# Two SwiGLU stages of a decoder layer: gate and up columns by seven block products over all of K, with one pool of raw weight buffers per stage

## The chip, the core and the metric

The kernel runs on one core of a Trainium2 chip. The core has five engines with instruction streams of their own: TensorE (PE, with its weight loads as PEld), VectorE (DVE), ScalarE (ACT), GpSimd (POOL) and SyncE (SP), which here issues most of the transfers. 16 DMA engines move data for the core. The metric is the device time of one execution in microseconds. A profile is one execution taken by the hardware profiler; its span runs from the first to the last instruction.

## What is computed

A decoder layer over 256 positions of width 2048: a SwiGLU half step, a mixer (dilated attention and gated linear attention), cross-attention into 256 memory tokens, and a second SwiGLU half step. All of it is in float32. The change concerns the two half steps:

```python
def swiglu(h, w_gate, w_up, w_down):
    return (jax.nn.silu(h @ w_gate) * (h @ w_up)) @ w_down

x = x + 0.5 * swiglu(rms_norm(x, ffn1_norm[l]), ffn1_w_gate[l], ffn1_w_up[l], ffn1_w_down[l])
...
x = x + 0.5 * swiglu(rms_norm(x, ffn2_norm[l]), ffn2_w_gate[l], ffn2_w_up[l], ffn2_w_down[l])
```

with D_MODEL = 2048 and D_FF = 5632. The row scale of the norm is put on after the products, so the products take x times the gain.

## The kernel before

**Weights.** Every weight is streamed from HBM once, in tiles of 128 partitions by 2048 float32 values (1 MiB, four k-blocks of 128 by 512 columns). A raw tile is worked on in two halves of 128 x 1024. ACT casts a half to fp32r (`wh`), DVE subtracts to get the remainder (`wl`, called a split below), and TensorE makes three matmuls of 512 columns per k-block and target: wh with xTh, wl with xTh, wh with xTl (lines 218 to 223, and 161 to 168 in the plain form). `wh` and `wl` have four buffers each (WB).

**An FFN** (line 376 on) goes through 11 chunks f of 512 columns. Chunk 0 makes gate and up plainly, 16 k-blocks each for two halves of the positions (t = 0, 1). In each later chunk, `seven` (line 257) makes gate and up of chunk f, and between its parts the chunk's code takes the `down` products of chunk f - 1, four per chunk, each 24 matmuls. Eight transposes turn the hidden values of chunk f - 1.

**The seven products.** Gate and up (two column blocks), the two halves of the positions, and two halves of a K block form a product of 2 x 2 blocks. `seven` makes it with seven products instead of eight. The weight quadrants of a block are loaded as T (gate, first K half), b21 (gate, second), b12 (up, first) and b22 (up, second). T is summed in place: T + b21, then + b12, then + b22, one sum ahead of each product that takes it. The seven products, each over all blocks, are in the prediction's names: **Y** (A21 with T + b21), **Z** ("22-21" with b21), **P2** ("12-21" with T), **R** (A12 with T), **P3** ("21-11" with b12), **X** ("22-12" with b22) and **P5** ("11-12" with b12 plus the gate's first quadrant, which an accumulating DMA adds into b12's buffer, `add_hbm`, line 209, on POOL's queue). "22-21" and the like are differences of blocks of x, made once in chunk 1 with DVE and ACT (`difference`, `x_differences`, delayed by `later`).

Before, a chunk has two such blocks and a rest. One block is 8 k-blocks (groups 0 and 1), one is group 2 cut in two (4 k-blocks, raw tiles of 512 KiB). Group 3 is plain (`plain`). That makes 84 + 42 + 48 = 174 matmuls for gate and up, and 96 of down: 270.

**Buffers.** `wp` is a pool that lives through all stages; its tag "raw" has four 1 MiB buffers (RB). An FFN stage adds a pool r of three (RX) and a pool q of four half tiles (RQ). A load waits on SP until its buffer's last readers are done. Stages are entered by `enter` (line 68), which closes the pools of the stage before.

**What sets the order.** The code is written in one order and a scheduler moves instructions by priorities: a lower-level block under `tc.high_priority(n)` is put earlier. WPRI = 200 is for splits and sums, LPRI = 260 for loads, FPRI = 300 for evictions (`urgent`, line 213). On each engine the resulting order is fixed: an instruction that waits holds all that stand behind it.

**Down.** The accumulators of `down` are filled beforehand by ACT with 2x, and evicted by ACT with a factor 0.5 (lines 420 on); those of chunk 0 aren't filled and are evicted by a DVE operation that adds x.

**Start.** The first three weight groups and input pieces are issued first (lines 120 to 133). Input pieces of one k-block are scaled by ACT, pieces of two by POOL (`packed`, line 321). 10 warm-up matmuls on a constant tile stand in the code (line 520).

Of the kernel before, what the change touches and what calls it, by code (L numbers as in the profile page):

```python
# [30 lines left out]
WARM = 10  # L31
# [12 lines left out]
UF = 18  # L44
UM = 34
SB = 7
RB = 4
RX = 3
RQ = 4
DIFF = 1  # L50
# [3 lines left out]
def layer_kernel(ctx: ExitStack, tc: tile.TileContext, A: dict, out: bass.AP):  # L54
# [25 lines left out]
    def enter_ffn():  # L80
        enter(2, down=2, u=UF, r=RX, q=RQ)
# [4 lines left out]
    def raw_tile(kind="raw"):  # L86

        if kind == "raw":
            return wp.tile([P, 4, 512], F32, tag="raw", name="raw", bufs=RB)
        return stage[kind].tile([P, 2 if kind == "q" else 4, 512], F32, tag=kind, name="raw")  # L90
# [46 lines left out]
    def wgroup(W, c, g, fine=None):  # L137
# [4 lines left out]
        with tc.high_priority(WPRI):  # L142
            if wload:
                raw = wload.pop(0)
            else:
                raw = wp.tile([P, kn, n], F32, tag="raw", name="raw", bufs=RB)
                SY.dma_start(raw, W[c, g])
# [40 lines left out]
    def load(src, kind="raw"):  # L188
        with tc.high_priority(ahead[0]):
            raw = raw_tile(kind)  # L190
            SY.dma_start(raw, src)
        return raw

    def parts(raw, n=4):

        for h in range(n // 2):
# [28 lines left out]
    def product(bank, form, raw, start, n):  # L225

        for h, half in enumerate(parts(raw, n)):
            mms(bank, form, half, start and h == 0, h == n // 2 - 1)
# [8 lines left out]
    PAIRS = {"22-21": ((1, 1), (1, 0)), "12-21": ((0, 1), (1, 0)), "22-12": ((1, 1), (0, 1)),  # L237
             "21-11": ((1, 0), (0, 0)), "11-12": ((0, 0), (0, 1))}

    def difference(x, name, n, home=None):  # L240

        a, b = PAIRS[name]
        with tc.high_priority(WPRI):
            d = W2([P, n, P], "d")
            V.tensor_sub(d, x[a], x[b])
            if home:
                hi, lo = home
            elif n == 4:
                hi, lo = (U([P, 4, P], F32R, nm) for nm in ("Fh", "Fl"))
            else:  # L250
                both = U([P, 4, P], F32R, "Fhl")
                hi, lo = both[:, 0:2], both[:, 2:4]
            SC.copy(hi, d)
            V.tensor_sub(lo, d, hi.bitcast(F32))
        return hi, lo

    def seven(blocks, ld, last, rest):
# [5 lines left out]
        T, b12, b21, b22 = [], [], [], []  # L263
        for i, (n, kinds, F, A12, A21) in enumerate(blocks):
            T.append(load(ld(i, 0, 0), kinds[0]))
            b21.append(load(ld(i, 1, 0), kinds[1]))
            add(T[i], b21[i])
            product(Y, A21, T[i], i == 0, n)
        urgent(SC.copy, Z, Y)
        yield "turn"  # L270
        for i, (n, kinds, F, A12, A21) in enumerate(blocks):
            product(Z, F["22-21"], b21[i], False, n)
        yield "down"
        for i, (n, kinds, F, A12, A21) in enumerate(blocks):
            b12.append(load(ld(i, 0, 1), kinds[2]))
# [4 lines left out]
        for i, (n, kinds, F, A12, A21) in enumerate(blocks):  # L280
            b22.append(load(ld(i, 1, 1), kinds[3]))
            add(T[i], b22[i])
            product(R, A12, T[i], i == 0, n)
        urgent(V.tensor_sub, X, R, sw)
        yield "down"
        for i, (n, kinds, F, A12, A21) in enumerate(blocks):
            product(Y, F["21-11"], b12[i], False, n)
            add_hbm(b12[i], ld(i, 0, 0))
        sv = W2([P, 512], "sv")
        urgent(SC.copy, sv, Y)  # L290
        urgent(V.tensor_sub, R, R, sv)
        for i, (n, kinds, F, A12, A21) in enumerate(blocks):
            product(X, F["22-12"], b22[i], False, n)
        plain((R, X), (rest(0), rest(1)), load(last(1)), (1, 0))
        yield "down"
        for i, (n, kinds, F, A12, A21) in enumerate(blocks):
            product(Y, F["11-12"], b12[i], False, n)
        yield "down"
        plain((Y, Z), (rest(0), rest(1)), load(last(0)), (0, 1))
        return Y, Z, R, X  # L300
# [20 lines left out]
    def packed(xr, k0, n, hi, lo, g0):  # L321

        if n == 1:
            SC.activation(xr[:, 0], xr[:, 0], AF.Copy, scale=gain[:, g0 + k0:g0 + k0 + 1])
        else:
            G.tensor_tensor(xr, xr, gain[:, g0 + k0:g0 + k0 + n].unsqueeze(2).broadcast_to([P, n, S]), op=ALU.mult)
        SC.copy(hi, xr)
        V.tensor_sub(lo, xr, hi.bitcast(F32))
# [47 lines left out]
    def ffn(pre, r, after, fine=None, last=False):  # L376
        wg, wu, wd = (A[f"{pre}_w_{n}"] for n in ("gate", "up", "down"))
        hT = {}
        F4, F2 = {}, {}
# [12 lines left out]
        def x4(t, c):  # L392

            return tuple(p[:, :, t * P:(t + 1) * P] for p in xT[c])

        def x2(t, c):

            return tuple(p[:, 2 * c:2 * c + 2, t * P:(t + 1) * P] for p in xT[2])

        def x_differences(block, n, F, some):  # L400

            if "xf" not in F:
                F["xf"] = {}
                for c in range(2):
                    for t in range(TT):
                        xf = F["xf"][t, c] = U([P, n, P], F32, "xf")
                        hi, lo = (p.bitcast(F32) for p in block(t, c))
                        with tc.high_priority(WPRI):
                            V.tensor_add(xf, hi, lo)
            homes = {"21-11": block(1, 1), "11-12": block(0, 0)}  # L410
            for name in some:
                F[name] = difference(F["xf"], name, n, homes.get(name))
# [6 lines left out]
        def down(f, c):  # L419

            acc = filled.pop() if filled else [stage["dn"].tile([P, 512], F32, tag="dn", name="dn") for _ in range(TT)]
            if last and f == NF - 1 and c == NC - 1:
                both = [w for half in wgroup(wd, c, f) for w in half]
                for t in range(TT):
                    mm3(acc, lhs_h, both, f == 0, True, (t,), skip_group_check=True)
            else:
                for h, half in enumerate(wgroup(wd, c, f)):
                    mm3(acc, lhs_h, half, f == 0 and h == 0, h == 1, skip_group_check=True)
                    tick()
            for t in range(TT):  # L430
                if f == 0:
                    urgent(V.scalar_tensor_tensor, xs[c][:, t], acc[t], 0.5, xs[c][:, t], op0=ALU.mult, op1=ALU.add)
                else:
                    urgent(SC.activation, xs[c][:, t], acc[t], AF.Copy, scale=0.5)
            f, c = (f, c + 1) if c < NC - 1 else (f + 1, 0)
            if 0 < f < NF:
                filled.append([stage["dn"].tile([P, 512], F32, tag="dn", name="dn") for _ in range(TT)])
                for t in range(TT):
                    urgent(SC.activation, filled[0][t], xs[c][:, t], AF.Copy, scale=2.0)

        hs = None
        for f in range(NF):
            todo = list(range(NC)) if f else []
            if f == 0:
# [3 lines left out]
                first, second = ("22-21", "12-21", "22-12"), ("21-11", "11-12")  # L448
                later(DIFF, lambda: x_differences(x4, 4, F4, first))
                later(DIFF + 2, lambda: x_differences(x2, 2, F2, first))  # L450
                later(DIFF + 5, lambda: x_differences(x4, 4, F4, second))
                later(DIFF + 6, lambda: x_differences(x2, 2, F2, second))
# [665 lines left out]
```

## Time and profile before

| what | us |
| --- | --- |
| median of three runs | 1919.14 |
| lowest and highest | 1918.01, 1919.18 |
| the profiled execution's own time | 1917.25 |
| its span | 1915.5 |
| DVE busy | 1471.9 |
| ACT busy | 1288.9 |
| second chunk of the first FFN, and of the second | 77.6, 67.2 |

How to read what the prediction quotes. A row of the windows view is a stretch of time: its length, the busy time of each engine in it with the number of instructions, the granted TensorE clock (1.00 is full), the mean busy share of the 16 DMA engines, and GB/s. A row of groups is one line of the kernel on one engine with the tile written and the tiles read, its shape, how often, busy time and mean ns, and the idle time before it with what ended it. A row of waits says which engine and line waited for which, the sum in us, how often, the longest. A row of the timeline or of the chain begins with its start in us and its length; a bracket at its end is the idle time before it and what ended that. DMA rows: a queue with packets, MB and its share of 16 engines (q1 is the queue of the loads that SP issues, q0 the one of the accumulating transfers that POOL issues), or an issue with its KB and the us from issue to landing.

The accumulating transfers' place in the whole run:

```profile
q1 hardware_dynamic: 62188, 370.74, 52.2%
q0 software_dynamic: 5760, 31.46, 8.8%
```

### The profile page before, as it was taken

Reading aid. Unit: us, or ns where it says so; the run is one execution under the profiler, and the core shown is the slowest. Engines: PE = TensorE matmul, PEld = TensorE weight load, DVE = VectorE, ACT = ScalarE, POOL = GpSimd, SP = SyncE. Lnnn points to the kernel's source line nnn. Section 1 sums busy time; section 2 is a strip of 40 time slices with the busy share of each in tenths; the row PEclk is TensorE's granted clock in tenths of the full one; section 3 lists DMA queues with packets and bytes.
Section 4 is the critical chain, followed back from the end, with each engine's and each line's share of the span. In section 5 each row is a group of like instructions: output and inputs, shape, how many; then the busy total and the mean of one; then the engine's idle time right before and its main releaser. Section 6 shows DMA issues by size and latency. Waiting matters only on the chain.

```text
span 1915.5 us, 22853 instructions
## 1 busy us (share of the span) xinstructions
PE 1892.8 (99%) x8640; PEld 1566.4 (82%) x8640; DVE 1471.9 (77%) x1499; ACT 1288.9 (67%) x1695; POOL 94.8 (5%) x101
## 2 busy tenths in 40 slices
PE   8899999999999999999999999999999999999999
PEld 6688888888888878778888889877888888888887
DVE  6987888788878865546785655898788878887884
ACT  6567777777777776444576545656777777777775
POOL 2000000000000000002220000000000000000000
PEclk9999999999999999999999999999999999999999
DMA  9577666776577444445466554747766677657743
GB/s 370 199 240 245 220 205 223 242 242 214 214 247 259 132 176 151 173 155 194 173 225 214 178 190 161 271 171 234 247 220 205 223 242 242 210 216 248 250 142 110
DMA packets 69211, 405.76 MB, mean 212 GB/s; under 512 B 7755, under 2 KB 8907, under 8 KB 28012
## 3 DMA queue, kind: packets, MB, share of 16 engines
q1 hardware_dynamic: 62188, 370.74, 52.2%
q0 software_dynamic: 5760, 31.46, 8.8%
q10 hardware_dynamic: 1152, 2.10, 0.3%
q8 instruction: 67, 1.10, 0.2%
q14 instruction: 44, 0.36, 0.1%
HBM read 402.17 MB, written 2.10 MB: 211 GB/s over the span
## 4 chain that ended last, share of the span: by engine, by line
PE 96%; DVE 2%; DMA 1%; ACT 1%; issue 0%; SPq 0%; DVEq 0%; ACTq 0%
PE acc L221 13%; PE acc L222 13%; PE acc L223 13%; PE acc L166 9%; PE acc L167 9%; PE acc L168 9%; PE dn L166 8%; PE dn L168 8%; PE dn L167 8%; DMA raw<-in_ffn_w_gate_dram 1%; PE tp L387 1%; DVE wl L202 1%; PE tp L344 1%; DVE raw L207 0%; PE dsp L697 0%
## 5 line engine op out<-in xcount | busy, mean ns | idle before, releaser
L201 ACT CAST wh<-raw 128x1024 fp32r<-128x1024 f32 x500 | 517.3, 1051 | 275.5 <-PE dn L168 103.8
L202 DVE TENSOR_TENSOR wl<-raw,wh 128x1024 fp32r<-128x1024 f32 x500 | 594.1, 1220 | 114.9 <-ACT wh L201 114.5
L158 DVE TENSOR_TENSOR wl<-raw,wh 128x1024 fp32r<-128x1024 f32 (+1 forms) x370 | 447.9, 1223 | 186.1 <-ACT wh L157 183.9
L157 ACT CAST wh<-raw 128x1024 fp32r<-128x1024 f32 (+1 forms) x370 | 384.9, 1048 | 205.3 <-PE acc L168 159.7
L222 PE MATMUL acc<-wl,xTh 128*128 128x512 f32 x800 | 313.2, 391 | 7.3 <-DVE wl L202 7.3
L221 PE MATMUL acc<-wh,xTh 128*128 128x512 f32 x800 | 312.7, 391 | 2.0 <-ACT wh L201 1.9
L223 PE MATMUL acc<-wh,xTl 128*128 128x512 f32 x800 | 312.7, 391 | 0.0
L166 PE MATMUL dn<-wh,hTh 128*128 128x512 f32 x704 | 274.7, 391 | 1.6 <-ACT hTh L303 1.1
L167 PE MATMUL dn<-wl,hTh 128*128 128x512 f32 x704 | 274.5, 390 | 0.5 <-DVE wl L158 0.5
L168 PE MATMUL dn<-wh,hTl 128*128 128x512 f32 x704 | 274.6, 390 | 0.0
L207 DVE TENSOR_TENSOR raw<-raw 128x2048 f32<-128x2048 f32 (+1 forms) x120 | 209.2, 1756 | 65.6 <-DMA raw<-in_ffn_w_gate_dram 64.1
L166 PE MATMUL acc<-wh,xTh 128*128 128x512 f32 x544 | 216.5, 398 | 6.4 <-ACT wh L157 6.4
L167 PE MATMUL acc<-wl,xTh 128*128 128x512 f32 x544 | 213.7, 393 | 0.0
L168 PE MATMUL acc<-wh,xTl 128*128 128x512 f32 x544 | 213.5, 392 | 0.0
L222 PEld LDWEIGHTS acc<-wl,xTh 128*128 128x128 f32 x800 | 150.8, 188 | 40.3 <-DVE wl L202 9.1
L221 PEld LDWEIGHTS acc<-wh,xTh 128*128 128x128 f32 x800 | 150.8, 189 | 34.1 <-ACT wh L201 2.8
L223 PEld LDWEIGHTS acc<-wh,xTl 128*128 128x128 f32 x800 | 150.8, 189 | 31.1
L166 PEld LDWEIGHTS dn<-wh,hTh 128*128 128x128 f32 x704 | 132.1, 188 | 30.9 <-ACT hTh L303 1.6
L167 PEld LDWEIGHTS dn<-wl,hTh 128*128 128x128 f32 x704 | 132.2, 188 | 28.2 <-DVE wl L158 1.1
L168 PEld LDWEIGHTS dn<-wh,hTl 128*128 128x128 f32 x704 | 132.2, 188 | 28.2 <-DVE hTl L304 0.9
L166 PEld LDWEIGHTS acc<-wh,xTh 128*128 128x128 f32 x544 | 103.0, 189 | 28.7 <-ACT wh L157 7.1
L167 PEld LDWEIGHTS acc<-wl,xTh 128*128 128x128 f32 x544 | 103.0, 189 | 21.6 <-DVE wl L158 0.9
(287 smaller groups left out, 2163.5 us busy)
## 6 DMA issues: line engine op xcount, KB each, us to landing
raw<-in_ffn_w_down_dram SPq DMA_DIRECT2D x88, 1024.0 KB, 6.5
raw<-in_ffn_w_up_dram SPq DMA_DIRECT2D x68, 1024.0 KB, 7.0
raw<-in_ffn_w_gate_dram SPq DMA_DIRECT2D x65, 1024.0 KB, 5.9
raw<-in_w_in_dram SPq DMA_DIRECT2D x48, 1024.0 KB, 4.8
raw<-in_ffn_w_gate_dram SPq DMA_DIRECT2D x44, 512.0 KB, 5.5
raw<-in_ffn_w_up_dram SPq DMA_DIRECT2D x40, 512.0 KB, 7.4
raw<-in_ffn_w_gate_dram POOLq DMA_DIRECT2D x20, 1024.0 KB, 8.7
raw<-in_w_out_dram SPq DMA_DIRECT2D x16, 1024.0 KB, 4.9
```

Of the source, the lines that this page charges most:

```text
L157: SC.copy(wh[:, d], src)
L158: V.tensor_sub(wl[:, d], src, wh[:, d].bitcast(F32))
L166: PE.matmul(acc[t], lh, wh, start=first and i == 0, stop=False, **kw)
L167: PE.matmul(acc[t], lh, wl, start=False, stop=False, **kw)
L168: PE.matmul(acc[t], ll, wh, start=False, stop=last and i == len(half) - 1, **kw)
L201: SC.copy(wh, src)
L202: V.tensor_sub(wl, src, wh.bitcast(F32))
L207: V.tensor_add(dst, dst, src)
L221: PE.matmul(bank, hi[:, k], wh, start=start and i == 0, stop=False, skip_group_check=True)
L222: PE.matmul(bank, hi[:, k], wl, start=False, stop=False, skip_group_check=True)
L223: PE.matmul(bank, lo[:, k], wh, start=False, stop=stop and i == len(half) - 1, skip_group_check=True)
L344: PE.transpose(tp[:, j], src[:, t, j * P:(j + 1) * P], ident)
```

## The change

- From chunk 2 on, both K halves of 1024 go by seven products: two blocks of 8 k-blocks, no rest. Chunk 1 has one such block and two plain groups. So a chunk has 168 matmuls of gate and up (180 in chunk 1).
- The raw buffers are one pool per stage: nine of 1 MiB in an FFN (RF), five in the mixer stage (RM). It is entered and closed with the stage.
- T's first sum of the first block goes by accumulating DMA (`hbm`), except in chunk 1 of the first FFN. b12's goes by it for both blocks. So a chunk has 3 MiB of accumulating transfers; it had 1.5.
- The differences of x are made where a product first asks for them (`Blocks`): the first block's in chunk 1, the second's in chunk 2.
- The order of the products changes: P3 stands ahead of R, with a down product between P2 and P3 and one between R and X.
- Down's accumulators of chunk 0 are filled too (with one matmul each that opens the bank); its eviction goes by ACT.
- At the start, 20 warm-up matmuls stand ahead, on a tile of x, and all input pieces are scaled by POOL.

```diff
-WARM = 10
+WARM = 20
...
-UF = 18
-UM = 34
-SB = 7
-RB = 4
-RX = 3
-RQ = 4
-DIFF = 1
+UF = 20
+UM = 36
+SB = 6
+RF = 9
+RM = 5
...
-        enter(2, down=2, u=UF, r=RX, q=RQ)
+        enter(2, down=2, raw=RF, u=UF)
...
+    def raw_tile():
+        return stage["raw"].tile([P, 4, 512], F32, tag="raw", name="raw")
...
+    class Blocks:
...
+        def __getitem__(self, name):
+            if name not in self.made:
+                if not self.sums:
+                    self.whole()
+                a, b = self.PAIRS[name]
+                with tc.high_priority(WPRI):
+                    d = W2([P, 4, P], "d")
+                    V.tensor_sub(d, self.sums[a], self.sums[b])
+                    hi, lo = self.home.get(name) or (U([P, 4, P], F32R, nm) for nm in ("Fh", "Fl"))
+                    SC.copy(hi, d)
+                    V.tensor_sub(lo, d, hi.bitcast(F32))
+                self.made[name] = (hi, lo)
+            return self.made[name]
+
+    def seven(F, ld, rest, hbm):
...
+        for i in N:
+            T.append(load(ld(i, 0, 0)))
+            if i in hbm:
+                add_hbm(T[i], ld(i, 1, 0))
+                b21.append(load(ld(i, 1, 0)))
             else:
...
+                b21.append(load(ld(i, 1, 0)))
+                add(T[i], b21[i])
+            product(Y, F[i].A21, T[i], i == 0)
         urgent(SC.copy, Z, Y)
         yield "turn"
...
+        for i in N:
+            product(Z, F[i]["22-21"], b21[i], False)
         yield "down"
...
+        for i in N:
+            b12.append(load(ld(i, 0, 1)))
             add(T[i], b12[i])
-            product(Y, F["12-21"], T[i], False, n)
+            product(Y, F[i]["12-21"], T[i], False)
         sw = W2([P, 512], "sw")
         urgent(SC.copy, sw, Y)
...
         yield "down"
...
+        for i in N:
+            product(Y, F[i]["21-11"], b12[i], False)
             add_hbm(b12[i], ld(i, 0, 0))
         sv = W2([P, 512], "sv")
         urgent(SC.copy, sv, Y)
...
+        b22 = []
+        for i in N:
+            b22.append(load(ld(i, 1, 1)))
+            add(T[i], b22[i])
+            product(R, F[i].A12, T[i], i == 0)
+        urgent(V.tensor_sub, X, R, sw)
+        urgent(V.tensor_sub, R if rest else sv, R, sv)
         yield "down"
...
+        for i in N:
+            product(X, F[i]["22-12"], b22[i], False)
+        for forms, src in rest:
+            plain((R, X), forms, load(src(1)), (1, 0))
         yield "down"
...
+        for i in N:
+            product(Y, F[i]["11-12"], b12[i], False)
...
-                if f == 0:
-                    urgent(V.scalar_tensor_tensor, xs[c][:, t], acc[t], 0.5, xs[c][:, t], op0=ALU.mult, op1=ALU.add)
-                else:
-                    urgent(SC.activation, xs[c][:, t], acc[t], AF.Copy, scale=0.5)
+                urgent(SC.activation, xs[c][:, t], acc[t], AF.Copy, scale=0.5)
...
+                rest = [([x_block(t, c) for t in range(TT)], lambda col, c=c: W[col][f, c]) for c in range(2 * n, NC)]
+                steps = seven(F[:n], lambda i, row, col: W[col][f, 2 * i + row], rest, () if first else (0,))
...
-    enter(4, u=UM)
+    enter(4, raw=RM, u=UM)
```

How the order moves. In the rows below a tile's number tells tiles of one name apart; `raw` is a raw weight tile, `wl` a split.

DVE, in a steady chunk of the first FFN before, from X's splits (raw_3704, raw_3727) to the sum for the next chunk (raw_4034, the next T, and raw_4036, its b21):

```order
L202 TENSOR_TENSOR wl_3837<-raw_3727,wh_3836 128x1024
L216 TENSOR_TENSOR acc_3536<-acc_3536,sv_3813 128x512
L202 TENSOR_TENSOR wl_3849<-raw_3846,wh_3848 128x1024
L202 TENSOR_TENSOR wl_3865<-raw_3846,wh_3864 128x1024
L158 TENSOR_TENSOR wl_3883<-raw_3880,wh_3882 128x1024
L158 TENSOR_TENSOR wl_3899<-raw_3880,wh_3898 128x1024
L202 TENSOR_TENSOR wl_3921<-raw_3666,wh_3920 128x1024
L207 TENSOR_TENSOR raw_4034<-raw_4034,raw_4036 128x2048
L202 TENSOR_TENSOR wl_3931<-raw_3666,wh_3930 128x1024
```

The same place after, where raw_3833 and raw_3856 are X's b22, raw_4076 and raw_4078 the second block's T and b21 of the next chunk, raw_3881 and raw_3961 the third and fourth down tile:

```order
L154 TENSOR_TENSOR wl_3884<-raw_3881,wh_3883 128x1024
L154 TENSOR_TENSOR wl_3900<-raw_3881,wh_3899 128x1024
L198 TENSOR_TENSOR wl_3922<-raw_3833,wh_3921 128x1024
L212 TENSOR_TENSOR acc_3550<-acc_3551,sw_3747 128x512
L212 TENSOR_TENSOR sv_3831<-acc_3551,sv_3831 128x512
L198 TENSOR_TENSOR wl_3932<-raw_3833,wh_3931 128x1024
L198 TENSOR_TENSOR wl_3942<-raw_3856,wh_3941 128x1024
L203 TENSOR_TENSOR raw_4076<-raw_4076,raw_4078 128x2048
L198 TENSOR_TENSOR wl_3952<-raw_3856,wh_3951 128x1024
L154 TENSOR_TENSOR wl_3964<-raw_3961,wh_3963 128x1024
```

The next chunk's large sum stood between P5's first two splits; now it stands ahead of the last split of X, the fourth down product's and P5's.

DVE ahead of the second down product's splits (raw_3741), before:

```order
L202 TENSOR_TENSOR wl_3670<-raw_3537,wh_3669 128x1024
L202 TENSOR_TENSOR wl_3680<-raw_3537,wh_3679 128x1024
L207 TENSOR_TENSOR raw_3562<-raw_3562,raw_3689 128x1024
L207 TENSOR_TENSOR raw_3537<-raw_3537,raw_3704 128x2048
L202 TENSOR_TENSOR wl_3693<-raw_3562,wh_3692 128x1024
L207 TENSOR_TENSOR raw_3562<-raw_3562,raw_3727 128x1024
L202 TENSOR_TENSOR wl_3708<-raw_3537,wh_3707 128x1024
L202 TENSOR_TENSOR wl_3718<-raw_3537,wh_3717 128x1024
L202 TENSOR_TENSOR wl_3731<-raw_3562,wh_3730 128x1024
L158 TENSOR_TENSOR wl_3744<-raw_3741,wh_3743 128x1024
```

and after (raw_3661 is the first down tile, raw_3749 the second):

```order
L154 TENSOR_TENSOR wl_3664<-raw_3661,wh_3663 128x1024
L154 TENSOR_TENSOR wl_3680<-raw_3661,wh_3679 128x1024
L203 TENSOR_TENSOR raw_3552<-raw_3552,raw_3701 128x2048
L203 TENSOR_TENSOR raw_3577<-raw_3577,raw_3724 128x2048
L198 TENSOR_TENSOR wl_3705<-raw_3552,wh_3704 128x1024
L198 TENSOR_TENSOR wl_3715<-raw_3552,wh_3714 128x1024
L198 TENSOR_TENSOR wl_3728<-raw_3577,wh_3727 128x1024
L198 TENSOR_TENSOR wl_3738<-raw_3577,wh_3737 128x1024
L203 TENSOR_TENSOR raw_3552<-raw_3552,raw_3833 128x2048
L154 TENSOR_TENSOR wl_3752<-raw_3749,wh_3751 128x1024
```

There are two whole tiles to sum for P2 now, and R's products stand behind the second down product instead of ahead of it; T's last sum of the first block has stayed ahead.

POOL's queue, accumulating transfers over some three chunks before (a whole and a half tile of b12 per chunk):

```order
L211 DMA raw_3169<-in_ffn1_w_gate_dram 128x2048
L211 DMA raw_3192<-in_ffn1_w_gate_dram 128x1024
L211 DMA raw_3666<-in_ffn1_w_gate_dram 128x2048
L211 DMA raw_3689<-in_ffn1_w_gate_dram 128x1024
L211 DMA raw_4163<-in_ffn1_w_gate_dram 128x2048
L211 DMA raw_4186<-in_ffn1_w_gate_dram 128x1024
```

and after, some two chunks (raw_3701 and raw_3724 are b12 of the chunk above, raw_4051 the next chunk's T of the first block):

```order
L207 DMA raw_3552<-in_ffn1_w_gate_dram 128x2048
L207 DMA raw_3225<-in_ffn1_w_gate_dram 128x2048
L207 DMA raw_3701<-in_ffn1_w_gate_dram 128x2048
L207 DMA raw_4051<-in_ffn1_w_gate_dram 128x2048
L207 DMA raw_3724<-in_ffn1_w_gate_dram 128x2048
L207 DMA raw_4200<-in_ffn1_w_gate_dram 128x2048
```

The next chunk's T stands between the two b12 transfers. On SP its load (raw_4051) is followed by those of raw_4054, raw_4076 and raw_4078, one after the other.

More of the change, by code (lines that the diff above doesn't have):

```diff
@@ L390, in turn, with x_block @@
                 hT[f, t] = (hi, lo)
-        def x4(t, c):
+        def x_block(t, c):
             return tuple(p[:, :, t * P:(t + 1) * P] for p in xT[c])
[L396 to L412, printed above, removed]
         def lhs_h(k, t):
@@ L518, in layer_kernel @@
     wps = PM([P, P], "wps")
-    for i in range(WARM):
-        PE.matmul(wps, idle, idle, start=True, stop=True)
+    with tc.high_priority(100000):
+        idle = xs[0][:, 0, 0:P]
+        V.memset(idle, -0.5)
+        for i in range(WARM):
+            PE.matmul(wps, idle, idle, start=True, stop=True)
     ident = con.tile([P, P], F32, name="ident")
```

132 lines of the change are left out of this document (53 added, 79 removed).

## The prediction

> **What bounds the kernel now.** I read the page first, then the windows of the steady chunks, TensorE's waits, and last the DMA queues between two chunks. From the page:
>
> ```profile
> span 1915.5 us, 22853 instructions
> PE 1892.8 (99%) x8640; PEld 1566.4 (82%) x8640; DVE 1471.9 (77%) x1499; ACT 1288.9 (67%) x1695; POOL 94.8 (5%) x101
> PE 96%; DVE 2%; DMA 1%; ACT 1%; issue 0%; SPq 0%; DVEq 0%; ACTq 0%
> ```
>
> TensorE is busy for 99% of the span and makes 96% of the chain that ended last. Next, a steady chunk of the first FFN by windows (length, busy PE, PEld, DVE, ACT, POOL, granted clock, DMA share, GB/s), the rows of the chain that begin it and the next one, and TensorE's two largest waits of the whole run:
>
> ```profile
> 320.69:382.84 62.15, 62.15 (x281) 51.58 (x279) 52.24 (x46) 45.95 (x56) 1.72 (x2) 1.00 0.67 229
> 320.69 0.87 PE tp L387 x8
> 382.84 0.87 PE tp L387 x8
> PE acc L222 <- DVE wl L202: 7.3, 4, 5.4
> PE acc L166 <- ACT wh L157: 6.4, 1, 6.4
> ```
>
> A chunk lasts 62.15 us at clock 1.00 and TensorE never waits in it. It has 270 matmuls of 512 columns beside the transposes, so one costs (62.15 - 0.87) / 270 = **0.227 us**, and each matmul saved is worth that, as long as nothing else becomes late. DVE works 52 of these 62 us. DMA looks idle for a third, but that is an average; here is its second between the accumulating transfers and the loads behind them (POOL's and SP's issues by the timeline; the issue views give us to landing; queue rows of 412 to 413, 414 to 415 and of 396 to 432 us; two windows):
>
> ```profile
> 404.80 0.86 POOL L211 DMA_DIRECT2D raw<-in_ffn_w_gate_dram  x1 [58.87 <-DVE wl L202]
> 407.51 0.86 POOL L211 DMA_DIRECT2D raw<-in_ffn_w_gate_dram  x1 [1.85 <-DVE wl L202]
> 411.24 1.47 SPq L191 DMA_DIRECT2D raw<-in_ffn_w_up_dram  x2
> 426.72 1.47 SPq L191 DMA_DIRECT2D raw<-in_ffn_w_up_dram  x2
> raw<-in_ffn_w_up_dram SPq DMA_DIRECT2D x1, 1024.0 KB, 7.7
> ...
> raw<-in_ffn_w_up_dram SPq DMA_DIRECT2D x1, 1024.0 KB, 5.0
> q0 software_dynamic: 55, 0.18, 96.4%
> ...
> q0 software_dynamic: 42, 0.14, 72.0%
> q1 hardware_dynamic: 16, 0.13, 32.2%
> q1 hardware_dynamic: 1246, 7.73, 57.0%
> q0 software_dynamic: 288, 1.57, 22.9%
> 408.00:410.00 2.00, 2.00 (x11) 1.65 (x10) 1.24 (x2) 2.00 (x4) 0.37 (x1) 1.00 1.04 209
> 420.00:422.00 2.00, 2.00 (x11) 1.65 (x10) 0.14 (x1) 1.05 (x1) 0.00 (x0) 1.00 1.00 418
> ```
>
> While an accumulation runs, all 16 DMA engines are full at half the bytes: 1 MiB costs 1.049 MB / 209 GB/s = 5.0 us against 2.5 for a load. By the queue rows it is 22.9% of 36 us for 1.5 MiB, or 5.5, against 2.8. I take 5.05 and 2.6, nearer to the windows, since the DMA share passes 1 where queue 0 runs alone (1.04 at 408). The first load issued at 411.24 has no packet up to 413; its queue appears at 414, as the accumulations end. It lands after 7.7 us, not 5.0 as the one issued at 426.72 does (I split the 5.0 into 0.95 to the first packet, 2.6 of work and 1.45 to landing). So a load **waits behind the accumulations issued before it**.
>
> **The change part by part**, all by these prices.
>
> Matmuls. From the third chunk on, 168 + 96 = 264 stand in place of 270; in the second, 276. Over both FFNs: 2 x (-9 x 6 + 6) = -96, or **-21.8 us**. The fills of the first down accumulators add 4 matmuls, **+0.9**. Without waits a chunk would last 264 x 0.227 + 0.87 = 60.8.
>
> DVE. Groups by form in three steady chunks, three splits in a row on the timeline, and ACT's cast for later:
>
> ```profile
> L202 DVE TENSOR_TENSOR wl<-raw,wh 128x1024 fp32r<-128x1024 f32 x76 | 90.4, 1221 | 19.3 <-ACT wh L201 19.3
> L207 DVE TENSOR_TENSOR raw<-raw 128x2048 f32<-128x2048 f32 x9 | 20.6, 2290 | 9.6 <-DMA raw<-in_ffn_w_gate_dram 9.5
> L216 DVE TENSOR_TENSOR acc<-acc,sw 128x512 f32<-128x512 f32 x3 | 2.1, 696 | 0.0
> ...
> 380.84 3.49 DVE L202 TENSOR_TENSOR wl<-raw,wh 128x1024 fp32r<-128x1024 f32 x3
> L157 ACT CAST wh<-raw 128x1024 fp32r<-128x1024 f32 x24 | 25.0, 1054 | 1.6 <-PE acc L223 1.6
> ```
>
> Back to back a split takes (3.49 - 1.22) / 2 = 1.135 and a large sum about 2.2. The new chunk has 36 splits (33 before) and 5 large sums (3 large and 3 half ones before), with six small operations of 0.6 to 0.7: 40.9 + 11.0 + 3.9 = 55.8 of 60.8 us. DVE isn't the bound, but what stands ahead of what now counts.
>
> The wait before the second down product. TensorE, from a chunk's first matmul (t = 0), runs Y to 5.45, transposes to 6.3, Z to 11.8, down to 17.2, P2 to 22.7 and the second down product from there. On DVE both sums of P2, its four splits and T0's last sum stand ahead of that product's splits; with the sums starting when the four splits of the first down product and Z are through, I get its first split about 0.7 late. Bounds: none, if the loads let the sums start earlier, to 1.25, one split. 16 chunks: **+11 [0, +20]**; cover gone is already in it.
>
> The wait in X: the large term. Shifted by 0.7, P3 runs 28.8 to 34.3, R to 39.7, the third down product to 45.2, X to 50.6. The nine buffers are then two T, two b12, two b22, two of down and the next T0, so each load of the next chunk waits for a last split. On SP, T0' is issued at 25.2 (after the second down product's last split), its partner at 34.1, T1' at 37.2, its partner at 39.5 (after the third down product's last split). The rule behind these: a half's cast waits for one of four buffers, that is for the matmuls of the fourth half before it, and cast and split follow (1.05 + 1.22). The third down product's second half so waits for R's second half, 34.3 + 12 x 0.227 = 37.0, and is split at 39.3, with small waits 39.5. On POOL the accumulations stand at 27.5 (b12, first block), 30.2 (T0', when its load has landed) and 32 (b12, second block): 3 MiB in place of 1.5, all ahead of three loads. DMA: T0' works from 26.15 to 28.75, the accumulations 3 x 5.05 to 43.9, the loads 3 x 2.6 to 51.7; the last lands at 53.15. The sum T1' + partner needs that load, and on DVE it stands right ahead of the split of X's fourth half. TensorE wants that split at 45.2 + 18 x 0.227 + 0.23 = 49.5, so DVE should begin the sum at 49.5 - 1.22 - 2.29 = 46.0, which allows 6.5 us from issue to landing. It begins 53.15 - 46.0 = 7.15 later, and behind it in DVE's order stand the fourth down product's and P5's splits, so TensorE stands for all of it. This recurs, since every issue here hangs on TensorE's own progress. Chunks 3 to 10 of each FFN, 16 in all: **+114**. By the two readings of DMA's price (5.0 and 2.5, 5.5 and 2.8) it is 6.5 and 8.6 each, 104 and 138; nothing at all, if loads passed. In the kernel before the same pattern had room, and once had too little:
>
> ```profile
> 423.27 2.29 DVE L207 TENSOR_TENSOR raw<-raw 128x2048 f32<-128x2048 f32 x1 [3.13 <-DMA raw<-in_ffn_w_gate_dram]
> 1309.65 2.29 DVE L207 TENSOR_TENSOR raw<-raw 128x2048 f32<-128x2048 f32 x1 [4.50 <-DMA raw<-in_ffn_w_gate_dram]
> PE acc L222 <- DVE wl L202: 0.6, 1, 0.6
> ```
>
> DVE idles 3.13 us for such a sum in a steady chunk, 4.50 in the second FFN's second chunk, where TensorE then loses 0.6.
>
> [...]
>
> Second and third chunk: the two FFNs' second chunks, and an idle stretch in the first:
>
> ```profile
> 56.52:134.16 77.64, 70.30 (x298) 56.23 (x297) 70.88 (x72) 45.63 (x51) 1.92 (x2) 0.96 0.57 193
> 1264.40:1331.63 67.23, 63.52 (x281) 51.41 (x280) 59.72 (x56) 38.65 (x42) 1.79 (x2) 1.00 0.64 211
> 62.00:66.00 4.00, 2.58 (x6) 2.10 (x7) 4.00 (x6) 0.34 (x1) 0.00 (x0) 0.50 0.00 0
> ```
>
> They last 15.5 and 5.1 above 62.15, while DVE makes all differences and the clock falls to 0.50. Now the first block's are made on demand in the second chunk, half the DVE work; that could return 7.5 and 2. But the second block's 14 operations of 0.6 to 0.7 come in the third, where DVE has 5 us left, at about +4 each. I take **0 [-10, +10]**.
>
> Start. The warm-up matmuls stand in the stream (behind them two early matmuls, the issue of the first group's fourth weight piece, and the landing of such pieces):
>
> ```profile
> 17.56 2.39 PE L520 MATMUL wps<-idle 128*128 128x128 f32 x20
> 13.03 0.63 PE L167 MATMUL acc<-wl,xTh 128*128 128x512 f32 x1
> 13.46 0.62 PE L168 MATMUL acc<-wh,xTl 128*128 128x512 f32 x1
> 4.48 0.43 SPq L133 DMA_DIRECT2D raw<-in_ffn_w_gate_dram  x1
> raw<-in_ffn_w_gate_dram SPq DMA_DIRECT2D x4, 256.0 KB, 5.1
> ```
>
> Ahead of everything they save 2.1 us, and the first matmuls may run at 0.23 instead of 0.43 apart; but ACT now casts all four weight pieces before the first input, and the fourth lands at 4.48 + 5.1 = 9.6; with its cast and an input's, together at most the 1.05 of a larger cast, the first real matmul slips from 6.4 to some 10.7. **-1.5 [-4, +3]**.
>
> Stages. Weight loads of the next stage used to start in a pool that outlived the stages:
>
> ```profile
> 687.08 7.83 SPq L147 DMA_DIRECT2D raw<-in_w_in_dram  x2
> 1186.79 18.45 SPq L147 DMA_DIRECT2D raw<-in_ffn_w_gate_dram  x4
> 1205.21 1.75 PE tp L344 x16
> ```
>
> The second FFN's were issued from 1186.79 on, while the stage before ran until 1205. Now they can start only after its last matmul: 5.0 to land and 1.05 for a cast, less 1.75 of transposes, is 4.3, with a split and a cold clock 6.5; the mixer's start 2.5. **+9 [+4, +16]**.
>
> Sum: -21.8 + 0.9 + 11 + 114 + 0 - 1.5 + 9 = **+111.6**. From the profiled execution's 1917.25 that is 2028.9; the median shown stands 1.9 above it, so **2031**.
>
> **The rivals.**
> [...]
> - *A light delay.* The next loads land in 7.7 to 9.5 us as they did behind 1.5 MiB, because the doubled accumulations spread out: 1.2 to 3.0 late, 19 to 48 in place of 114: 1936 to 1965. For it: no row shows 3 MiB in a burst.
> - *Faster.* The loads pass the accumulations, and the partner of T1' lands in under 6.5 us, as the 5.0 at 426.72; the term of 114 is gone. What is left is 2031 - 114 = 1917, and 1906 where early loads take the wait before the down product as well; 1911 in the middle. It decides at 6.5 us from issue to landing.
> - *Not what it says.* The matmuls are counted from the program's order and can't come out otherwise; only their gain can be eaten, as above.
>
> **How the numbers follow.** Chances: the wait as reckoned 0.51 (own range 1990 to 2054), turns 0.12, light delay 0.17, faster 0.17, worse than 2054 0.03. A measurement can tell about 0.2%, 4 us, from no change, so of the 0.17 I give 0.12 to faster and 0.05 to the same; the rest, 0.83, is slower. The range takes in the first three, 1936 to 2054, and leaves out 0.20.
>
> **What would show it.** Right: chunks of about 68.7 us, with one wait of 7 us of X's matmuls for DVE's split, DVE idle ahead of the large sum for the gate load, queue 0 full for 15 us in one stretch and 3 MiB of it per chunk, and loads behind it landing in 13 to 18 us. Wrong: chunks near 61 with such loads landing in 5 to 6 us (faster), or at 62.5 to 64 with 8 to 9 (light delay). The second FFN should begin with an idle TensorE of 4 to 7 us. If the wait stands at the second down product instead, DVE's order there is the cost, not DMA.

## The result and the profile after

The changed kernel takes **2102.45 us** (median of four, 2100.59 to 2106.93) beside 1919.06 of the kernel before (1918.01 to 1919.18): a ratio of **1.096**, 95% interval 1.0941 to 1.0979. It is slower, as forecast, but by 183 us in place of 112, and lies above the range of 1936 to 2054.

From the page of the kernel after: the span, busy times, and the chain that ended last.

```profile
span 2101.3 us, 22761 instructions
PE 1930.8 (92%) x8568; PEld 1575.3 (75%) x8568; DVE 1536.3 (73%) x1506; ACT 1344.6 (64%) x1771; POOL 113.0 (5%) x122
PE 51%; DVE 20%; DMA 13%; ACT 8%; issue 7%; SPq 0%; POOL 0%; DVEq 0%; ACTq 0%; POOLq 0%
```

The span grew by 185.8 us. TensorE's idle time grew from 22.7 to 170.5, or by 147.8. Its busy time also *grew*, by 38.0, although it does 92 matmuls of 512 columns fewer. So there are two costs to find: waits, and slower matmuls. First, the waits view: TensorE's largest waits in the whole run (sum in us, how many, the longest).

```profile
PE acc L218 <- DVE wl L198: 128.0, 16, 9.0
PE acc L217 <- ACT Fh L265: 12.9, 3, 4.8
PE dn L163 <- DVE wl L154: 4.9, 17, 1.0
```

The windows of chunks 1, 2 and 6 of the first FFN (counted from 0 as in the code):

```profile
58.52:134.37 75.85, 70.62 (x305) 56.94 (x303) 61.43 (x60) 50.02 (x63) 1.92 (x2) 0.98 0.60 196
134.37:214.32 79.95, 66.93 (x273) 53.52 (x272) 62.42 (x60) 51.18 (x64) 2.58 (x3) 0.89 0.62 197
430.42:502.17 71.75, 63.43 (x273) 51.47 (x272) 56.69 (x48) 48.38 (x59) 2.59 (x3) 0.95 0.68 220
```

There are 16 waits of 8.0 us on average (7.1 to 9.0), one in each chunk that was to have one. A steady chunk lasts 71.75 us in place of 62.15, at a mean granted clock of 0.95. The third chunk of each FFN stands out with 80. Now one steady chunk around its wait: on the timeline SP's and POOL's issues, DVE's late sum with the split behind it, and the matmul that waited.

```profile
450.40 14.84 SPq L187 DMA_DIRECT2D raw<-in_ffn_w_gate_dram  x4
...
455.84 0.86 POOL L207 DMA_DIRECT2D raw<-in_ffn_w_gate_dram  x1 [2.04 <-DMA raw<-in_ffn_w_gate_dram]
457.69 0.86 POOL L207 DMA_DIRECT2D raw<-in_ffn_w_gate_dram  x1 [0.99 <-DVE wl L198]
...
479.40 2.29 DVE L203 TENSOR_TENSOR raw<-raw 128x2048 f32<-128x2048 f32 x1 [9.12 <-DMA raw<-in_ffn_w_gate_dram]
481.61 1.22 DVE L198 TENSOR_TENSOR wl<-raw,wh 128x1024 fp32r<-128x1024 f32 x1
...
482.88 0.80 PE L218 MATMUL acc<-wl,Fh 128*128 128x512 f32 x1 [7.92 <-DVE wl L198]
```

The chain goes through the same place with one long piece:

```profile
464.91 14.40 DMA raw<-in_ffn_w_gate_dram
```

TensorE stands 7.92 us for a split. The split is behind a large sum on DVE, which itself waits 9.12 us for the last of the four gate loads, issued at 464.91 and 14.40 us on its way. This chunk's transposes begin at 430.42 and Y's 24 matmuls (5.45 us) lie ahead of them, so t = 0 of the prediction's ledger is 424.97. The ledger put that last issue at 39.5, and it came at 39.9. It put the accumulations at 30.2 and 32, and they came at 30.9 and 32.7.

The windows view of the same stretch shows the second cost:

```profile
469.00:474.00 5.00, 5.00 (x24) 4.15 (x23) 1.23 (x1) 4.53 (x8) 0.00 (x0) 1.00 1.00 277
474.90:482.90 8.00, 0.08 (x2) 0.02 (x1) 3.50 (x3) 0.92 (x1) 0.00 (x0) 0.80 0.69 292
482.90:486.40 3.50, 3.50 (x8) 2.81 (x9) 3.33 (x3) 0.98 (x1) 0.00 (x0) 0.50 0.67 232
486.40:490.00 3.60, 3.60 (x17) 2.92 (x16) 1.38 (x2) 1.12 (x2) 0.00 (x0) 0.99 1.01 401
```

TensorE is busy without a gap in the third row, but gets through 8 matmuls in 3.5 us; in the row behind it is 17 in 3.6. The granted clock has fallen to 0.50 in the idle stretch and stays there after it.

### The profile page after: what moved, and what is told of

Read it like the earlier page. It is cut to its first block, busy times and chain, and to the rows that moved or that the text cites. A ratio compares the mean times of both kernels' runs of the same rounds, so it can differ in the third digit from the quotient of the medians.

```text
span 2101.3 us, 22761 instructions
## 1 busy us (share of the span) xinstructions
PE 1930.8 (92%) x8568; PEld 1575.3 (75%) x8568; DVE 1536.3 (73%) x1506; ACT 1344.6 (64%) x1771; POOL 113.0 (5%) x122
## 4 chain that ended last, share of the span: by engine, by line
PE 51%; DVE 20%; DMA 13%; ACT 8%; issue 7%; SPq 0%; POOL 0%; DVEq 0%; ACTq 0%; POOLq 0%
DMA raw<-in_ffn_w_gate_dram 12%; DVE wl L198 9%; PE acc L162 8%; PE acc L163 8%; PE acc L164 8%; PE dn L163 5%; PE dn L164 5%; DVE wl L154 5%; PE dn L162 5%; ACT wh L197 4%; DVE raw L203 4%; PE acc L218 4%; PE acc L219 3%; PE acc L217 3%; ACT x L212 1%
## 5 line engine op out<-in xcount | busy, mean ns | idle before, releaser
L198 DVE TENSOR_TENSOR wl<-raw,wh 128x1024 fp32r<-128x1024 f32 x548 | 653.9, 1222 | 127.0 <-ACT wh L197 123.5
L203 DVE TENSOR_TENSOR raw<-raw 128x2048 f32<-128x2048 f32 x95 | 216.0, 2288 | 158.3 <-DMA raw<-in_ffn_w_gate_dram 158.0
L218 PE MATMUL acc<-wl,Fh 128*128 128x512 f32 x456 | 190.6, 418 | 128.0 <-DVE wl L198 128.0
L217 PE MATMUL acc<-wh,xTh 128*128 128x512 f32 x672 | 263.7, 392 | 4.0 <-ACT sw L212 4.0
L218 PE MATMUL acc<-wl,xTh 128*128 128x512 f32 x672 | 261.8, 390 | 0.0
L219 PE MATMUL acc<-wh,xTl 128*128 128x512 f32 x672 | 261.8, 390 | 0.0
L162 PE MATMUL acc<-wh,xTh 128*128 128x512 f32 x544 | 216.1, 398 | 7.3 <-ACT xTh L347 3.7
L164 PE MATMUL acc<-wh,xTl 128*128 128x512 f32 x544 | 213.5, 393 | 0.0
L163 PE MATMUL acc<-wl,xTh 128*128 128x512 f32 x544 | 213.3, 392 | 0.0
L218 PEld LDWEIGHTS acc<-wl,Fh 128*128 128x128 f32 x456 | 91.0, 200 | 154.1 <-DVE wl L198 134.7
L217 PE MATMUL acc<-wh,Fh 128*128 128x512 f32 x456 | 186.7, 409 | 16.5 <-ACT Fh L265 12.9
L219 PE MATMUL acc<-wh,Fl 128*128 128x512 f32 x456 | 187.9, 412 | 0.2 <-DVE Fl L266 0.2
L217 PEld LDWEIGHTS acc<-wh,xTh 128*128 128x128 f32 x672 | 126.2, 188 | 37.0 <-ACT sw L212 11.6
## 6 DMA issues: line engine op xcount, KB each, us to landing
raw<-in_ffn_w_gate_dram SPq DMA_DIRECT2D x85, 1024.0 KB, 12.2
raw<-in_ffn_w_gate_dram POOLq DMA_DIRECT2D x57, 1024.0 KB, 11.7
```

The source lines that it names most:

```text
L162: PE.matmul(acc[t], lh, wh, start=first and i == 0, stop=False, **kw)
L163: PE.matmul(acc[t], lh, wl, start=False, stop=False, **kw)
L164: PE.matmul(acc[t], ll, wh, start=False, stop=last and i == len(half) - 1, **kw)
L198: V.tensor_sub(wl, src, wh.bitcast(F32))
L203: V.tensor_add(dst, dst, src)
L217: PE.matmul(bank, hi[:, k], wh, start=start and i == 0, stop=False, skip_group_check=True)
```

## The experiments

Every edit starts from the changed kernel or from e1, and runs beside the kernel before on the same chip. Ratios are to that kernel.

**e1: the late sum behind X's and down's splits.** Nothing is changed but DVE's order, by way of two tiny operations on GpSimd:

```diff
+        return half[-1][2]
...
+    mark = []
...
+                if i and mark:
+                    held = ST(1, "held")
+                    G.tensor_tensor(held, T[i][:, 0, 0:1], mark[0], op=ALU.add)
                 add(T[i], b21[i])
...
-            product(Y, F[i]["11-12"], b12[i], False)
+            wl = product(Y, F[i]["11-12"], b12[i], False)
+            if i == 0:
+                mark[:] = [ST(1, "mark")]
+                G.tensor_tensor(mark[0], wl[:, 0:1].bitcast(F32), mhalf[:, 0:1], op=ALU.add)
```

> The second block's first sum for the next chunk is tied, by two tiny GpSimd operations, to the split of P5's second half, so that on DVE it stands behind X's and the fourth down product's splits. No transfer is changed. Theory (an instruction order that holds splits behind a late sum): the 16 waits of X, 128 us, go, and the half-speed stretch behind each with them, 16 x about 2 = 32: 2102 - 160 = about 1940 (1925 to 1955), with the loads still landing 13 to 15 us after issue. Rival (the transfers set the pace): TensorE waits for the same data at the next chunk's Y, in about the same length: above 2085.

Measured: **1936.76 us**, ratio 1.0094 (1.0079 to 1.0109). The page's row of busy times:

```profile
PE 1895.3 (98%) x8568; PEld 1554.0 (80%) x8568; DVE 1537.2 (79%) x1506; ACT 1344.9 (69%) x1771; POOL 119.8 (6%) x160
```

A steady chunk by windows:

```profile
388.74:450.59 61.85, 61.47 (x273) 50.26 (x272) 56.77 (x48) 48.42 (x59) 2.97 (x5) 1.00 0.78 255
```

In that chunk, the sum on the timeline:

```profile
437.84 2.29 DVE L203 TENSOR_TENSOR raw<-raw 128x2048 f32<-128x2048 f32 x1 [1.06 <-DMA raw<-in_ffn_w_gate_dram]
```

The sum still waits for its load, and the two last loads still need a median of 14.2 us to land. But what stands behind the sum now is needed later, and the chunk lasts 61.85 us at clock 1.00. The same transfers in the same time cost nothing: the X wait is one of **order on DVE**, and the rival that the transfers set the pace falls for 3 MiB. With the same matmuls, TensorE is busy for 1930.8 - 1895.3 = 35.5 us less than after the change. This is the price of the half clock: in the changed kernel's trace the clock stays at 0.50 for 3.0 to 5.9 us behind each of the sixteen waits, 68.7 us in all, and half of that, 34 us, is lost work.

**e2: four accumulations per chunk, no first sum on DVE at all.**

```diff
-                steps = seven(F[:n], lambda i, row, col: W[col][f, 2 * i + row], rest, () if first else (0,))
+                steps = seven(F[:n], lambda i, row, col: W[col][f, 2 * i + row], rest, () if first else range(n))
```

> The second block's first sum goes by accumulating transfer too: 4 MiB of such transfers per chunk in place of 3, and no first sum on DVE. Theory (order on DVE): X's waits go although DMA has 1 MiB more of accumulation, since 12 x 2.6 + 4 x 5.05 = 51 us of transfers still fit into 61: 1940 (1925 to 1960). Rival (the transfers set the pace): the accumulation adds 5 us per chunk to the wait, at the next chunk's Y: above 2150.

Measured: **2004.91 us**, ratio 1.0450 (1.0434 to 1.0466): both expectations missed. X's waits went, but waits came at the next chunk's Y. The waits around one Y of this kernel (325 to 337 us):

```profile
PE acc L218 <- DVE wl L198: 1.6, 2, 0.8
PE acc L217 <- ACT wh L197: 1.1, 1, 1.1
```

On the timeline, the issue of the fourth accumulation that this Y takes:

```profile
318.19 0.86 POOL L207 DMA_DIRECT2D raw<-in_ffn_w_gate_dram  x1 [18.99 <-DVE wl L198]
```

The fourth accumulation can only be issued when its own load has landed. This load was issued at 303.28 and landed 14.4 us later; 0.56 us behind that comes the accumulation's issue, in all eight such chunks of the first FFN (the bracket names a split that ends in the same half microsecond). The accumulation takes 12.1 us more. So it comes some 1 us too late for the cast. Over the whole run TensorE waits 21.6 us for such casts and 19.8 for splits, and is busy for 24.6 us more than in e1. At 4 MiB the rival is right in kind, though not in size: not the sum of DMA's work decides, which fits, but two late transfers in a row.

**e3: two accumulations per chunk**, with `()` in place of `() if first else (0,)` in the line above.

> No first sum goes by accumulating transfer: 2 MiB of them per chunk in place of 3, one large sum more on DVE. Theory (loads behind accumulations, order on DVE): the loads get through about 5 us earlier, X's wait shrinks from 8.0 to about 3.0, with up to 1 us more where the other sum precedes X's first split: 2102 - 16 x 4.5 = about 2030, down to 1990 if the clock no longer falls behind the shorter waits. Rival (DVE's load sets the wait): one sum more makes it longer, above 2102.

Measured: **2005.87 us**, ratio 1.0454 (1.0438 to 1.0470), between the two values that the theory gave. In a steady chunk of 65.74 us TensorE waits 1.9 us for splits and 1.1 us for the subtraction that opens X (`PE acc L217 <- DVE acc L212`). So 3.0 us is left, as expected, but not in the place that was expected: the sum that was late before finds its load there, and it is the other sum, the first block's, that now waits 3.84 us for its load and holds X's subtraction and first splits. Fewer accumulations ahead made the wait shorter (3.0 us in place of 8.0) although DVE had more to do (58.61 us busy in this chunk, 56.69 in the one shown of the changed kernel).

**e4: the wait filled with matmuls.**

```diff
...
+            if h and fill:
+                idle = PM([P, 512], "idle")
+                for _ in range(fill):
+                    PE.matmul(idle, form[0][:, half[0][0]], half[0][1], start=True, stop=True)
             mms(bank, form, half, start and h == 0, h == 1)
...
-            product(X, F[i]["22-12"], b22[i], False)
+            product(X, F[i]["22-12"], b22[i], False, FILL if i and more else 0)
...
```

> 34 matmuls of 512 columns, whose result nobody reads, stand ahead of the last half of X and fill its wait. Theory (the clock falls after the idle time): the sum and the split come when they came before, the granted clock stays at 1.00 and the matmuls behind run at 0.227 apart: 16 x 1.6 to 2.5 us less, about 2068 (2060 to 2078). Rival (TensorE is slowed behind the wait by something else, such as late operands): 2102, or more.

Measured: **2074.45 us**, ratio 1.0810 (1.0792 to 1.0828): 28.0 us less than the changed kernel, within the range. A steady chunk by windows:

```profile
425.78:496.81 71.03, 69.52 (x308) 56.57 (x306) 56.59 (x48) 48.42 (x59) 2.59 (x3) 1.00 0.69 222
```

Its largest wait:

```profile
PE acc L219 <- DVE wl L199: 1.1, 1, 1.1
```

34 matmuls more in each of the sixteen chunks make the kernel faster. The data come when they came before, and the clock stays at 1.00. So the idle time itself brings the slow matmuls behind it. This chunk is 0.7 us shorter than the one shown above, as its fill ends 1.1 us too early; the sixteen chunks are shorter by 1.75 us on average.

**e5, on e1: R's sums behind the second down product's splits**, by the same two operations (`done` from down's split, `held` ahead of `add(T[i], b22[i])`).

> e1, and R's two sums (T's third ones) are tied behind the second down product's splits in the same way. Theory (DVE's order costs the second down product's start about 0.6 to 1.05 us in each of 16 chunks): 1936.8 - 10 to 17 = 1920 to 1927. Rival (the gaps there are TensorE's wait for ACT's copy of Y, 0.2 us each, and no matter of sums): 1933 to 1938.

Measured: **1925.08 us**, ratio 1.0032 (1.0020 to 1.0045): 11.7 less than e1. A steady chunk lasts 61.17 us by windows:

```profile
446.67:507.84 61.17, 61.17 (x274) 50.26 (x272) 56.59 (x48) 48.51 (x59) 5.28 (x8) 1.00 0.78 258
```

**e6, on e1: five of the nine buffers in a pool that is kept.**

```diff
...
-        return stage["raw"].tile([P, 4, 512], F32, tag="raw", name="raw")
+        k = count[0] % RF
+        count[0] += 1
+        pool = stage["raw"] if k >= RM and "raw" in stage else wp
+        return pool.tile([P, 4, 512], F32, tag="raw", name="raw", bufs=RM if pool is wp else RF - RM)
...
```

> e1, and five of the nine raw buffers lie in a pool that lives through all stages (four more in the FFN stages), so that the next stage's loads may start before the stage ends. Theory (pools closed at a stage's end cost the mixer's and the second FFN's start what the stretch between the two FFNs grew by, 582.4 - 574.6 = 7.7 us): 1929 to 1933. Rival (the stretch grew for other reasons, such as one small buffer less): 1936.8 within 2.

Measured: **1987.14 us**, ratio 1.0356 (1.0342 to 1.0371), which neither expected. Two neighbouring chunks of it by windows:

```profile
332.66:392.34 59.68, 58.88 (x262) 47.92 (x260) 52.37 (x44) 43.50 (x54) 3.18 (x5) 1.00 0.83 264
392.34:465.55 73.21, 68.98 (x285) 55.22 (x285) 61.51 (x52) 54.18 (x64) 2.98 (x5) 0.93 0.66 216
```

Two pools of five and four don't do what one of nine does. The chunks became uneven, and the second FFN's first gate loads came to stand behind its up loads. The stretch between the FFNs stayed at 583.0 us. The experiment says nothing on what a kept pool is worth; the question is open.

**e7, on e1: the old way of scaling the first input pieces, and 10 warm-up matmuls**, still ahead of all.

> e1, with the one-block input pieces scaled by ACT again and 10 warm-up matmuls in place of 20, still ahead of all. Theory (ACT's casts of four weight pieces ahead of the first input hold the first real matmul): the first transposes come at about 56.5 or earlier in place of 58.7, 1933 to 1935. Rival (the start is set by the loads, or by the clock): 1936.8 within 1.

Measured: **1934.70 us**, ratio 1.0081 (1.0067 to 1.0095): 2.1 less than e1. The first transposes come at 52.56 in place of 58.73, but the chunk behind them takes 76.93 in place of 74.75. Of the 4 us that should be left by the two profiles, the medians show half, and as the two intervals overlap, that gain is not clear of noise.

**e8, on e1: three of a block's five differences one chunk earlier.**

```diff
...
                 up = proj(wu, f, lhs_x, range(4))
+            if f < 2:
+                for name in ("22-21", "12-21", "22-12"):
+                    F[f][name]
```

> e1, with three of the five differences of each block made one chunk ahead of their use (the first block's in chunk 0, the second's in chunk 1). Theory (making them where they are asked for holds TensorE and costs the second and third chunks together some 15 us over both FFNs): 1922 to 1930, the third chunks at 62 to 65 in place of 69.7 and 68.8. Rival (DVE's work only moves a chunk ahead, where DVE has no room): 1936 or more.

Measured: **1916.92 us**, ratio 0.9987 (0.9978 to 0.9996): 19.8 less than e1, and more of a gain than the theory's 1922 to 1930. The third chunk of the first FFN in e1, and then in e8:

```profile
133.48:203.19 69.71, 64.69 (x273) 52.07 (x272) 62.32 (x60) 51.23 (x64) 2.96 (x5) 0.95 0.69 226
```

```profile
128.21:192.90 64.69, 63.15 (x278) 51.04 (x277) 60.68 (x55) 51.65 (x64) 2.96 (x5) 1.00 0.74 244
```

The 12.9 us of waits for `Fh` are gone, and the clock of 0.95 with them. The third chunks last 64.69 us in both FFNs, as expected; the second ones, 74.75 and 69.90 in e1, have become shorter too, 68.41 and 65.84.

**e9: e5, e7 and e8 together.**

> e5, e7 and e8 together on e1. If their gains add up: 1936.8 - 11.7 - 2.1 - 19.8 = 1903 (1900 to 1908), below the kernel before. Rival (the gains overlap, since the early differences and the sums behind the down product want the same room on DVE): 1910 to 1917.

Measured: **1906.82 us**, ratio 0.9933 (0.9921 to 0.9946): faster than the kernel before by 0.67%. The gains add up but for 4 us. The page's row of busy times:

```profile
PE 1884.4 (99%) x8548; PEld 1548.3 (81%) x8548; DVE 1530.7 (80%) x1506; ACT 1347.4 (71%) x1775; POOL 158.4 (8%) x210
```

A steady chunk by windows:

```profile
436.36:497.59 61.23, 61.23 (x274) 50.27 (x273) 56.62 (x48) 48.54 (x59) 5.31 (x8) 1.00 0.78 258
```

**e10: the changed kernel without b12's accumulations**, the line `add_hbm(b12[i], ld(i, 0, 0))` taken out.

> The changed kernel without b12's accumulating transfers (P5 takes b12 alone, so gate lacks its first quadrant's part); the order on DVE and on SP is the changed kernel's. Theory (the sum is late because its load stands behind accumulations): the load lands 5 to 6.5 us after issue, X's waits and the half-speed stretches behind them go: 1936 to 1946. Rival (the sum is late through its place in DVE's order alone, whatever the transfers do): X's wait stays at 4 us or more, above 2030.

Measured: **1952.03 us**, ratio 1.0169 (1.0153 to 1.0184). This is 6 us above the theory's 1936 to 1946, and far from the rival's 2030. The sum, in the same place on DVE, now comes with its load after 6.5 us (median of the gate loads; 12.2 in the changed kernel). On the timeline:

```profile
435.14 2.29 DVE L203 TENSOR_TENSOR raw<-raw 128x2048 f32<-128x2048 f32 x1 [1.50 <-DMA raw<-in_ffn_w_gate_dram]
```

The limit that the prediction gave was 6.5 us from issue to landing, and waits of 0.3 to 2.0 us are left in eleven chunks, 10.5 in all. With e1 the cause has both its halves. Either the accumulations ahead of the load or the sum's place ahead of X's split has to go, and the wait goes with it.

## Why the prediction was wrong, and what it had right

| term | predicted | measured | from |
| --- | --- | --- | --- |
| matmuls and fills | -20.9 | -14.4 | chunks 3 to 10 of both FFNs, e5 less before |
| wait in X | +114 | +128.0 | waits of the changed kernel |
| half clock behind it | 0 | +35.5 | busy PE, changed kernel less e1 |
| second down product | +11 | +11.7 | e5 less e1 |
| second and third chunks (differences) | 0 | +14.0 | e1 less before |
| start | -1.5 | +2.0 | first transposes, after less before |
| stages | +9 | +6.5 to 7.7 | stretch between the FFNs, after and e1 |

The column comes to 183 to 185, beside 185.8 of the spans. Its rows are taken from different runs, so the sum is a check on the whole and not on each row.

**What bounds, and the price of a matmul.** Right in kind: without its waits (e5) the new chunk is TensorE's busy time. It lasts 61.17, where the prediction had 60.8 and the kernel before has 62.15. So six matmuls fewer saved 0.98 us a chunk, not 1.36; what takes the rest isn't shown.

**The wait in X.** Right in its place, its cause and its count, and 14 us too small: 8.0 in place of 7.15 each. The last gate load was issued 0.4 us later than reckoned and landed at t = 479.3 - 424.97 = 54.3 in place of 53.15. The price of a transfer was a little low: by the DMA view of 420 to 492 us, 1 MiB took 5.3 us of all 16 engines when accumulated and 2.7 when loaded, where 5.05 and 2.6 were reckoned, and with these the ledger gives 54.4. (By the ledger's own steps its dearer reading, 5.5 and 2.8, gives a wait of about 9 us and some 147 in all, not the 8.6 and 138 that stand there.)

**The step that failed** is "TensorE stands for all of it", priced by the wait's length alone. Each idle stretch of 8 us here also halved the clock of what came next, to 0.50. That is 35.5 us, half of what was missed (74); e4, which fills the stretches, gives 28.0 of it back. With this term the sum would have been about 2066, still short of 2102: the rest is the wait in X, the differences and the matmuls. A row that says so stood in the prediction, the 0.50 of 62 to 66 us behind the first FFN's idle stretch, but it was used for the second chunk only and not for the sixteen new waits. The row of 482.90 to 486.40 shows it again: 3.5 us at 0.50, with 8 matmuls. In the sixteen waits the clock fell 2.2 to 5.2 us after TensorE had become idle and rose 3.0 to 5.9 us after it was busy again: no fixed length is seen here.

**Differences on demand** is the second term that was mis-sized: 0 was chosen between -10 and +10. In e1, where X no longer waits, the second chunk of the first FFN and the second and third of the second FFN are these; the first FFN's third, 69.71 us, is shown at e8.

```profile
58.73:133.48 74.75, 70.73 (x304) 57.32 (x303) 61.65 (x60) 50.00 (x63) 2.31 (x4) 0.95 0.61 198
1277.23:1347.13 69.90, 68.08 (x299) 55.14 (x298) 57.09 (x57) 49.01 (x62) 2.10 (x4) 1.00 0.65 211
1347.13:1415.93 68.80, 63.78 (x274) 51.48 (x273) 62.42 (x60) 51.23 (x64) 2.96 (x5) 0.95 0.70 229
```

Together the four last 283.2 us; before, 77.64 and 67.23 for the second chunks and twice the steady 62.15 make 269.2, which is 14.0 less. The prediction counted DVE's room in the third chunk. What it cost is that a product waits for a chain of sum, difference, cast and split from the moment it asks (three waits of 3.3 to 4.8 us, and a mean clock of 0.95 in three of these four chunks). The 19.8 of e8 is more than this 14.0, since making three of the five differences earlier also brings the second chunks below those of the kernel before.

**Start and stages.** Small, the start with the wrong sign but inside its bounds: the first real matmul did slip, to 11.44 us, and the gain behind it was smaller than that, so the first transposes come at 58.52 in place of 56.52. The second FFN began with a wait of 3.7 us for a cast, where the prediction had 4 to 7; that the pool's closing causes it was not shown (e6).

**The rivals.** A light delay, 1.2 to 3.0 us a chunk, is what 2 MiB of accumulations bring (e3, 3.0 in the chunk read above), not 3 MiB; with 1 MiB (e10) it is at most 2.0. The faster case was named rightly by what decides it: e10 meets the limit of 6.5 us and the large wait goes. But its time was out of reach here, 1952 and 1937 (e1) in place of 1911, through the terms above. Turns, to which the prediction gave 0.12, need a closer look: did the loads run together with the accumulations? The DMA view's queue rows of the changed kernel, for 460 to 461 and then 470 to 471 us (packets, MB, share of 16 engines).

```profile
q0 software_dynamic: 39, 0.20, 112.7%
...
q0 software_dynamic: 17, 0.14, 66.7%
q1 hardware_dynamic: 16, 0.12, 30.5%
```

The loads, the first issued at 460.0, had no packets up to 464, as the prediction had it. Then, up to 474, both queues ran, about packet for packet, as the two rows of 470 to 471 show. So the two queues shared the engines from 464 to 474 us and not from 460 to 464. That did not help the loads: a packet of an accumulation took about twice the time of a load's there (17 packets for 66.7% against 16 for 30.5%), and the last load landed 1.2 us later than the prediction's strict order has it.

## What to carry to other kernels

Reckon with an instruction's place in its engine's order, not with the engine's share: DVE was 73% busy, and one sum a chunk that waited for a late load held TensorE for 128 us. Price a TensorE wait of several us by more than its length: the matmuls behind the waits of 8 us ran at a clock of 0.50 here, and that added more than a quarter to them (35.5 us to 128.0). Before a transfer is moved to another queue, add up what will stand ahead of the transfers that the next sum needs, and look at which work queues behind that sum.

## What the runs showed of the hardware

After idle stretches of 8 us the granted clock stayed at 0.50 for 3.0 to 5.9 us of matmuls (3.5 in the chunk shown), and filling sixteen such stretches with 34 useless ones each made the kernel 28 us faster (e4). Behind e10's eleven waits of 0.3 to 2.0 us for a split the matmuls were 0.22 to 0.24 us apart from the second on, and its chunk of 393.76 to 456.21 us, with a wait of 0.3, kept a clock of 1.00. Loads issued behind accumulating transfers had no packets for about 4 us, and then shared the DMA engines with the last of them, in the row shown at 30.5% for the loads and 66.7% for the accumulation; what decides when the sharing begins was not tested.
